# First feed-forward block: w1, w3 and gate in two passes that store w2's operands, then w2 alone as seven half-size products over all 1280 tokens

## The chip, the cores and the metric

The kernel runs on one core of a Trainium2 chip, one launch per execution. The metric is the time of one execution in microseconds (us). The kernel before takes 3238.82 us, the median of three runs from 3236.75 to 3240.59 us. The times of the rows below are of one profiled execution of it, which took 3245.91 us; the profile's span inside it is 3242.6 us, so that 3.3 us lie around the span.

## The reference

Two layers over 1024 latent tokens and 256 context tokens, D = 1024, all in fp32. Each layer has a mixer (layer 0: a state space beside latent attention; layer 1: retention beside HGRN2) and then a SwiGLU feed-forward block of 2816 hidden columns. The change is in the block of layer 0, where both streams are computed:

```python
def swiglu(h, w1, w3, w2):
    return (jax.nn.silu(h @ w1) * (h @ w3)) @ w2
...
        x = x + gx2 * swiglu(rms_norm(x, norm2_g[li]) * (1.0 + ax2) + sx2, ffn_w1[li], ffn_w3[li], ffn_w2[li])
        if not last:
            ...
            ctx = ctx + gc2 * swiglu(rms_norm(ctx, norm2_g[li]) * (1.0 + ac2) + sc2,
                                     ffn_w1[li], ffn_w3[li], ffn_w2[li])
```

The factors gx2 and gc2 (one number per column) are slices of the modulation vectors, one set for latent and one for context tokens. Behind this block comes the RMSNorm of layer 1, which every projection of layer 1 reads.

## The kernel before

**Numbers and products.** Every fp32 operand of a large product is split into a high and a low part (`split`, L175: ScalarE rounds the high part, L177; VectorE subtracts it, L43), and a product is three TensorE matmuls: high by high, high by low, low by high. Activations lie with features on the 128 partitions and tokens along the row. The 1280 tokens are held in two halves of 640: `x[0]` has 640 latent tokens, `x[1]` 384 latent and 256 context tokens (`HSEGS`).

**w1 and w3 as seven half-size products.** `Ffn.pair(j)` (L1292) does two of the 22 blocks of 128 hidden columns. Its 256 columns, the 1024 inputs and the 640 tokens of a half are each cut in two, and `seven` (L1243) makes the 2x2 block product from seven products of half size instead of eight (Strassen-Winograd). Each is 12 matmuls of 128x128 weights by 320 tokens (L1258). The seven sums of weights are cut for every pair (`wset`: four sums on GpSimd, seven splits of 512 columns); the seven sums of the input, the operands `ops` of 4x320, are cut once per half (`combos`, L1177, 14 pieces of 640). VectorE and GpSimd add up the results; `gate` multiplies silu(w1 part) by the w3 part, 128x320 at a time, and splits the result (`gh`, `gl`).

**w2 inside the pairs.** `Ffn.w2` (L1329) multiplies the gate of the pair before, 256 hidden columns deep, by the rows of w2: for 8 output blocks of 128 and two token segments (384 and 256) two times three matmuls, 96 in all (L215 to L217), and one `scalar_tensor_tensor` (L46) per output block and segment that scales the result and adds it to x. Thus x is read and written 11 times per half. The program issues it between the w1 and the w3 of the next pair; behind the last pair of a half it stands alone.

**Order.** The first pass does `x[0]`, the second `x[1]`. During the first, `prep` normalizes `x[1]` piece by piece; at the change of passes `combos` cuts the operands of the second pass, which takes the place of those of the first. During the second pass the sums of squares and the norm of `x[0]` for layer 1 are made; behind it stand the last w2, its sums of squares, and the norm of the first segment of `x[1]`; its second segment is normed after the first projection of layer 1. Beside the pairs TensorE also makes layer 1's modulation vectors (`mod_groups`, tile `psmod`). The order on each engine is set by a scheduler, except inside `tc.manual_schedule`, where the engines named take the program's order. SyncE (`Q`) issues all loads and stores, in one queue.

**The second block.** The block of layer 1 (1024 tokens) already works in the other way, with the class `Gate` (L1376): its `pair` does w1, w3 and the gate, sums the gate's four quarters into the seven operands of w2 on GpSimd, and hands each to `store`; behind the last pair w2 runs alone, as seven products over all its tokens, with its operands read back from DRAM.

## Time and profile before

| | us |
|---|---|
| median of three runs | 3238.82 |
| profiled execution | 3245.91 |
| span of the profile | 3242.6 |
| TensorE busy | 3045.4 (94% of the span) |
| VectorE busy | 2113.4 (65%) |
| GpSimd busy | 1352.8 (42%) |
| ScalarE busy | 1321.8 (41%) |
| first feed-forward block, first to last matmul | 858.9 to 1798.7: 939.8 |

The trace is read in microseconds from the span's start. Engines are PE (TensorE matmul), PEld (its weight loads, which overlap it), DVE (VectorE), ACT (ScalarE), POOL (GpSimd) and SP (SyncE). A row names the line of the kernel, the engine, the operation, and the tile written and the tiles read by the program's names. Tiles of `flat` that serve again keep their first names: `mh` and `ml` as outputs of a split, or as operands of a matmul, are in this block operands of `ops` or slots of the ring of weights. TensorE's busy time includes stretches in which the throttle granted it a lower clock; "granted clock" is the share of full speed.

### The profile page before, as it was taken

The numbers are of one execution on the slowest core, as the hardware profiler recorded it, in microseconds if no ns is written. First come the engines' busy times: TensorE is split into PE (matmuls) and PEld (weight loads), VectorE is DVE, ScalarE is ACT, GpSimd is POOL, SyncE is SP. The second block draws the span as 40 slices with busy tenths as digits, with TensorE's granted clock in tenths as the row PEclk, the third lists the DMA queues.
The fourth block names the chain that finished last, engine by engine and source line by source line (L and its number), as shares of the span: only waits on it lengthen the run. The fifth ranks groups of instructions, "written<-read, shape, count | busy, mean of one in ns | idle before, by whom it ended". The sixth has DMA issues, their size and how long they took to land.

```text
span 3242.6 us, 49888 instructions
## 1 busy us (share of the span) xinstructions
PE 3045.4 (94%) x19010; PEld 2727.4 (84%) x19010; DVE 2113.4 (65%) x3431; ACT 1321.8 (41%) x2643; POOL 1352.8 (42%) x1251
## 2 busy tenths in 40 slices
...
GB/s 247 271 162 112 17 19 28 115 163 189 124 118 111 111 116 99 140 108 118 104 118 66 66 33 33 40 43 40 40 44 197 98 95 102 103 101 102 332 214 140
DMA packets 168104, 363.10 MB, mean 112 GB/s; under 512 B 29865, under 2 KB 62265, under 8 KB 167097
## 3 DMA queue, kind: packets, MB, share of 16 engines
...
q14 instruction: 90, 0.74, 0.1%
...
## 4 chain that ended last, share of the span: by engine, by line
PE 67%; DVE 8%; issue 5%; POOL 4%; ACT 4%; DMA 2%; SPq 0%; POOLq 0%; ACTq 0%; DVEq 0%
PE psf L1412 13%; PE psf L1258 11%; PE psu L215 5%; PE psu L216 5%; PE psu L217 5%; PE psf L215 2%; PE psf L216 2%; PE psf L217 2%; PE pso L217 2%; PE pso L216 2%; PE pso L215 2%; PE psl L1751 2%; PE pso L2033 2%; PE pso L2035 2%; PE pso L2034 2%
## 5 line engine op out<-in xcount | busy, mean ns | idle before, releaser
L215 PE MATMUL psu<-mh,wh 128*128 128x384 f32 (+1 forms) x1024 | 327.3, 320 | 1.7 <-ACT qr L1629 1.2
L217 PE MATMUL psu<-mh,wl 128*128 128x384 f32 (+1 forms) x1024 | 323.8, 316 | 0.0
L216 PE MATMUL psu<-ml,wh 128*128 128x384 f32 (+1 forms) x1024 | 323.0, 315 | 0.0
L1412 PE MATMUL psf<-mix,ring 128*128 128x512 f32 x1248 | 295.7, 392 | 0.8 <-DVE c L43 0.8
L1412 PEld LDWEIGHTS psf<-mix,ring 128*128 128x128 f32 x1248 | 234.4, 188 | 53.2 <-DVE c L43 1.2
L43 POOL TENSOR_TENSOR fsum<-fraw,fsum 128x512 f32<-128x512 f32 x64 | 99.7, 1558 | 234.1 <-DVE ml L43 105.3
L215 PEld LDWEIGHTS psu<-mh,wh 128*128 128x128 f32 x1024 | 194.7, 190 | 2.2 <-ACT qr L1629 1.4
L216 PEld LDWEIGHTS psu<-ml,wh 128*128 128x128 f32 x1024 | 194.6, 190 | 0.1
L217 PEld LDWEIGHTS psu<-mh,wl 128*128 128x128 f32 x1024 | 194.3, 190 | 0.1
L46 DVE SCALAR_TENSOR_TENSOR x<-psf,mod,x 128x384 f32<-128x384 f32 (+1 forms) x352 | 175.1, 540 | 24.3 <-PE psf L217 20.7
L43 POOL TENSOR_TENSOR fsum<-fraw 128x512 f32<-128x512 f32 x75 | 108.1, 1442 | 130.8 <-DMA fraw<-ffn_w 99.7
L43 DVE TENSOR_TENSOR ml<-fraw,ml 128x512 fp32r<-128x512 f32 x132 | 125.7, 952 | 37.8 <-ACT ml L177 35.9
L43 POOL TENSOR_TENSOR s<-s,c 128x320 f32<-128x320 f32 x60 | 74.1, 1235 | 173.0 <-DVE c L43 164.3
L43 DVE TENSOR_TENSOR wx<-pT,wx 128x512 fp32r<-128x512 f32 x168 | 113.1, 682 | 33.4 <-ACT wx L836 33.4
L1258 PE MATMUL psf<-opx,mh 128*128 128x320 f32 x792 | 134.0, 310 | 0.8 <-DVE mh L43 0.8
L1412 PE MATMUL psf<-opx,ring 128*128 128x512 f32 x528 | 131.4, 393 | 2.2 <-ACT pu L1443 2.2
L829 ACT ACTIVATE pt<-pss,st 128x512 f32<-128x512 f32 (+1 forms) x208 | 123.5, 604 | 13.5 <-DVE st L817 11.5
L43 DVE TENSOR_TENSOR wl<-wraw,wh 128x1024 fp32r<-128x1024 f32 x61 | 90.4, 1481 | 59.0 <-ACT wh L177 49.0
L1258 PE MATMUL psf<-opx,ml 128*128 128x320 f32 x792 | 128.6, 310 | 0.2 <-DVE ml L43 0.2
L177 ACT CAST ml<-fraw 128x512 fp32r<-128x512 f32 x132 | 81.7, 619 | 111.0 <-PE psf L1258 33.7
L43 POOL TENSOR_TENSOR acc<-acc,sq 128x384 f32<-128x384 f32 (+2 forms) x57 | 71.7, 1264 | 132.3 <-ACT sq L1129 119.0
L43 POOL TENSOR_TENSOR xa<-xa,tot 128x1280 f32<-128x1280 f32 x24 | 87.2, 3634 | 90.2 <-ACT ku L1743 75.8
...
## 6 DMA issues: line engine op xcount, KB each, us to landing
...
```

The source lines that it names most:

```text
L43: return e.tensor_tensor(out=out, in0=in0, in1=in1, op=op)
L46: return V.scalar_tensor_tensor(out=out, in0=in0, scalar=scalar, in1=in1, op0=op0, op1=op1)
L177: S.copy(out=hi, in_=src)
L215: PE.matmul(ps, wh, xh, start=start, stop=False)
L216: PE.matmul(ps, wh, xl, start=False, stop=False)
L217: PE.matmul(ps, wl, xh, start=False, stop=stop)
L829: S.activation(out=o, in_=ps, func=AF.Exp, bias=st, accum_out=dd)
L1258: PE.matmul(ps, u[:, k], v[:, k], start=start and k == 0 and j == 0, stop=(k == 3 and j == 2), skip_group_check=True)
L1412: PE.matmul(ps(n), u[:, k], v[:, k], start=start and k == 0 and j == 0, stop=(k == 3 and j == 2), skip_group_check=True)
L1751: PE.matmul(ps[:, c], ku[:, c], qu, start=True, stop=True)
L2033: PE.matmul(o, wh, h, start=first, stop=False, skip_group_check=True)
L2034: PE.matmul(o, wh, l, start=False, stop=False, skip_group_check=True)
```

## The change

The class `Ffn` goes; the first block uses `Gate` as the second does. What each part does:

- **Pairs.** For each half and pair: w1 and w3 as seven products each, with products in the order 0, 5, 1, 3, 2, 4, 6. The gate runs on VectorE for all four quarters; GpSimd makes six sums of 128x320 a pair, two of results and four of the gate's quarters. Three quarters as they are and these four sums are w2's seven operands; each, 164 KB, is stored to a DRAM tile `g_d0` (154 stores in all; those of the very last pair are issued during w2's first product). No w2 in the pairs and no update of x.
- **Pass change.** The first weights of the second pass are cut between the pieces of `combos` (`get`), in the order in which the products take them.
- **w2.** Seven products over all 1280 tokens. The 2816 hidden columns come as 11 chunks j; each of products 0, 5, 1, 3, 2, 4 takes for each chunk one sum of w2's rows (`w2_op`, one split of 512) and one operand of 640 tokens (`x_op`: a load from `g_d0` and a split of 640), and runs 24 matmuls of 320 into eight PSUM banks (4 output blocks, 2 halves). The last three chunks go bank by bank, and behind each bank `put` adds the sum to x by `scalar_tensor_tensor`, once for each of the four quarters of a half that the product enters (`PUT`); in `x[1]`'s second 320 tokens as 64 latent and 256 context tokens. Product 6 runs the two halves one after the other. The sum t of the weights of products 1, 2, 3 is made in product 1, stored to `t_d` and read again in 2 and 3; its stores are issued two at a time.
- **Norms.** The sums of squares for layer 1 move into products 4 and 6; the norm of `x[0]` stands in the second half of product 6, both norms of `x[1]` behind layer 1's first projections of `x[0]` (two, then three column segments).
- **Order.** TensorE's and SyncE's orders in the w2 part are those of the program.

On TensorE, at the change from the first pass to the second. Before: `psf` by L1258 are w1 and w3 products, `gh` and `gl` the gate that w2 reads (L215, L216).

```order
L1258 MATMUL psf_12991<-mh_6900 128x320 x12
L1258 MATMUL psf_12990<-mh_6900,ml_6901 128x320 x12
L1258 MATMUL psf_12990<-ml_6901 128x320 x12
L215 MATMUL psf_13146<-gh_12697,mh_6900 128x384
L215 MATMUL psf_13147<-gh_12697,mh_6900 128x256
L215 MATMUL psf_13148<-gh_12697,mh_6900 128x384
L215 MATMUL psf_13149<-gh_12697,mh_6900 128x256
```

After (L1276 is the matmul of `Gate`; a product is twelve matmuls with one `psf`):

```order
L1276 MATMUL psf_11732<-opx_7473,mh_6900 128x320 x4
L1276 MATMUL psf_11492<-ml_6901,mh_6900 128x320 x12
L1276 MATMUL psf_11732<-ml_6901 128x320 x12
L1276 MATMUL psf_11760<-opx_7473,mh_6900 128x320 x2
L1276 MATMUL psf_11788<-opx_7473,ml_6901 128x320 x8
L1276 MATMUL psf_11613<-mh_6900 128x320 x12
L1276 MATMUL psf_11788<-opx_7473,ml_6901 128x320
L1276 MATMUL psf_11760<-opx_7473,mh_6900 128x320 x10
L1276 MATMUL psf_11788<-opx_7473,ml_6901 128x320 x3
L1276 MATMUL psf_11852<-opx_7473,ml_6901 128x320 x10
L1276 MATMUL psf_11613<-ml_6901 128x320 x12
L1276 MATMUL psf_11852<-opx_7473,ml_6901 128x320 x2
```

In the first listing the pass's last product is followed by matmuls of w2 on the last gate, so that TensorE has 96 of them between the passes; in the second the last product of the first pass is followed at once by products of the second.

On GpSimd, inside one pair. Before: `fsum` and `fraw` are sums of weights (512), `s`, `c` and `pu` sums of results (320).

```order
L43 TENSOR_TENSOR fsum_12565<-fraw_12563 128x512
L43 TENSOR_TENSOR fsum_12566<-fsum_12565,fraw_12561 128x512
L43 TENSOR_TENSOR fraw_12563<-fraw_12561,fraw_12563 128x512
L43 TENSOR_TENSOR fsum_12565<-fraw_12561,fsum_12566 128x512
L43 TENSOR_TENSOR s_12272<-pu_12306,pu_12304 128x320
L43 TENSOR_TENSOR fsum_12703<-fraw_12701 128x512
L43 TENSOR_TENSOR fsum_12704<-fsum_12703,fraw_12699 128x512
L43 TENSOR_TENSOR fraw_12701<-fraw_12699,fraw_12701 128x512
L43 TENSOR_TENSOR fsum_12703<-fraw_12699,fsum_12704 128x512
L43 TENSOR_TENSOR s_12272<-s_12272,c_12273 128x320
L43 TENSOR_TENSOR c_12273<-pu_12591,pu_12589 128x320
L43 TENSOR_TENSOR s_12272<-s_12272,c_12273 128x320
```

After (the same names; `c` holds sums of the gate as well):

```order
L43 TENSOR_TENSOR fsum_13096<-fraw_13084 128x512
L43 TENSOR_TENSOR s_12810<-s_12810,pu_12873 128x320
L43 TENSOR_TENSOR fsum_13100<-fsum_13096,fraw_13082 128x512
L43 TENSOR_TENSOR fraw_13084<-fraw_13082,fraw_13084 128x512
L43 TENSOR_TENSOR fsum_13096<-fraw_13082,fsum_13100 128x512
L43 TENSOR_TENSOR fsum_13234<-fraw_13088 128x512
L43 TENSOR_TENSOR c_12811<-c_12811,pu_13013 128x320
L43 TENSOR_TENSOR fraw_13088<-fraw_13086,fraw_13088 128x512
L43 TENSOR_TENSOR fsum_13238<-fsum_13234,fraw_13086 128x512
L43 TENSOR_TENSOR c_12811<-s_12810 128x320
L43 TENSOR_TENSOR s_12810<-s_12810 128x320
L43 TENSOR_TENSOR c_12811<-c_12811,s_12810 128x320
```

Each pair keeps its four sums of weights for w1 and four for w3; the sums of results with `pu` are fewer, and sums of the gate's quarters (`c` and `s` alone) stand between the sums of weights.

On SyncE, at the start of product 1 of w2. Before there is no such stage; the nearest is a pair, where rows of w2 are loaded between other weights.

```order
L1220 DMA fraw_16730<-ffn_w2 128x1024
L1220 DMA fraw_16732<-ffn_w2 128x1024
L1220 DMA fraw_16870<-w_mod 128x1024
L1220 DMA fraw_16872<-w_mod 128x1024
L1220 DMA fraw_16874<-w_mod 128x1024
L1220 DMA fraw_16888<-ffn_w3 128x1024
L1220 DMA fraw_16890<-ffn_w3 128x1024
```

After (`mh` here is a slot that takes a chunk's operand from `g_d0`; `t_d` takes the sums kept for products 2 and 3):

```order
L1379 DMA fraw_15506<-ffn_w2 128x2x512
L1380 DMA fraw_15507<-ffn_w2 128x512
L1496 DMA mh_6900<-g_d0_8576 128x640
L1379 DMA fraw_15543<-ffn_w2 128x2x512
L1380 DMA fraw_15544<-ffn_w2 128x512
L1496 DMA mh_6900<-g_d0_8576 128x640
L1531 DMA t_d_14754<-fsum_15509 128x512
L1531 DMA t_d_14754<-fsum_15546 128x512
L1379 DMA fraw_15582<-ffn_w2 128x2x512
L1380 DMA fraw_15583<-ffn_w2 128x512
```

A chunk of product 1 has two loads of w2 and one of an operand; two stores of t stand ahead of the loads of every second chunk.

```diff
...
                 split(S, ops[i][0][:, k], ops[i][1][:, k], src[:, k])
+            get(i)
 
         def sub(out, in0, in1):
             for k in kk:
         sub(b12, b12, b11)
         yield
         cut(0, b11)
+        cut(5, b21)
         cut(1, b12)
         sub(b12, b22, b12)
+        cut(3, b22)
         cut(2, b12)
         sub(b11, b12, b11)
-        cut(3, b22)
+        cut(4, b11)
         sub(b12, b21, b12)
-        cut(4, b11)
-        cut(5, b21)
         cut(6, b12)
-    class Ffn:
...
-        def pair(self, j):
...
-            self.w2()
...
-            def gate(i, v):
-                tt(G if i and j < NF // 2 - 1 else V, s[:, i], s[:, i], v, ALU.mult)
-                split(S, g[0][:, i], g[1][:, i], s[:, i])
...
     ORDER = (0, 5, 1, 3, 2, 4, 6)
     W2_ORDER = (0, 2, 5, 4, 1, 6, 3)
 
-    def w2_op(l, i, j, raw, fsum, slot, stash):
+    def w2_op(l, i, j, raw, fsum, slot, stash, keep=None):
         wh, wl = slot[:, 0:512], slot[:, 512:1024]
         w = a["ffn_w2"][l, 2 * j * P:(2 * j + 2) * P].rearrange("(f p) c -> p f c", p=P)
-        t = stash and stash[:, 512 * j:512 * j + 512]
         rr = lambda: raw().rearrange("p (f k) c -> p f (k c)", f=2)
         r = rr()
-        if i in (0, 5, 6, 1, 3):
+        if l == 0 and i in (1, 2, 3):
+            if i == 1:
+                r2, src, t = rr(), fsum(), fsum()
+                Q.dma_start(out=r, in_=w[:, :, 512:])
+                Q.dma_start(out=r2[:, 0], in_=w[:, 0, 0:512])
+                tt(G, src, r[:, 0], r[:, 1], ALU.add)
+                tt(G, t, src, r2[:, 0], ALU.subtract)
+                keep(j, t)
+            elif i == 2:
+                src = r[:, 0]
+                Q.dma_start(out=src, in_=stash[j])
+            else:
+                src = r[:, 0]
+                Q.dma_start(out=src, in_=w[:, 1, 0:512])
+                Q.dma_start(out=r[:, 1], in_=stash[j])
+                tt(G, src, src, r[:, 1], ALU.subtract)
...
     wp = tc.alloc_tile_pool(name="w5b", bufs=1, reuse_waits="tile")
-    f = Ffn(0, 320, HSEGS, ops, itertools.cycle(rs), wp, fr, pp,
-            lambda raw: mod_groups(1, raw, pp))
-    cb = combos(x[1], 320, ops, xs_d[1])
-    f.run(0, x[0], itertools.chain([0], prep(0, 3, 4, x[1], accs[1], HSEGS[1], xs_d[1], pp), itertools.islice(cb, 1)))
-    next(cb)
-    f.w2()
-    acc = Acc(xpool[0], HSEGS[0])
-    f.run(1, x[1], itertools.chain(stats(acc, HSEGS[0], x[0], wp),
-                                   prep(1, 0, 1, x[0], acc, HSEGS[0], x_d[:, :, 0:HALF[0]], pp)))
+    fraw = lambda: fr.tile([P, KT, P], F32, name="fraw", bufs=4)
+    f = Gate(0, 320, ops, itertools.cycle(rs), fraw)
+    f.pools(wp, wp, pp)
+    NJ = NF // 2
+    g_d = dram.tile([7, NJ, P, 2, 320], F32, name="g_d0")
+    fill = mod_groups(1, f.raw, pp)
+    store = lambda p, j: lambda i, v: Q.dma_start(out=g_d[i, j, :, p], in_=v)
+    w1 = [None]
+    cb = combos(x[1], 320, ops, xs_d[1], lambda i: w1[0].get(i))
+    mid = itertools.chain([0], prep(0, 3, 4, x[1], accs[1], HSEGS[1], xs_d[1], pp), itertools.islice(cb, 1))
+    kept = []
+    for p, j in itertools.product(range(2), range(NJ)):
+        keep = (lambda i, v: kept.append((i, v))) if p and j == NJ - 1 else store(p, j)
+        f.pair(j, keep, (w1[0], None), lambda: 0 < j < NJ - 1 and next(fill, None))
+        w1[0] = None
+        if p == 0:
+            next(mid, None)
+            if j == NJ - 1:
+                w1[0] = f.wset("ffn_w1", 0)
+                next(cb)
+    wp.release()
...
+    xslots = [itertools.cycle(v), itertools.cycle(v[6:]), itertools.cycle(slots([(bx, 0, 3200)], 640, 5))]
+    t_d = dram.tile([NJ, P, 512], F32, name="t_d")
     hh, hl = halves(HALF[0])
-    f.ring = iter(rs[6:])
-    w2 = f.w2_load()
-    for k in range(KT):
-        S.copy(out=hh[0][:, k], in_=x[0][:, k])
-        tt(G if k % 2 else V, hl[0][:, k], x[0][:, k], hh[0][:, k].bitcast(F32), ALU.subtract)
-    acc = Acc(xpool[0], HSEGS[1])
-    with tc.manual_schedule(engines={PE.engine}):
-        for i, d in itertools.product(range(2), range(KT)):
-            if i or d > 3:
-                f.w2_units(w2, [(i, d)])
-            elif d == 0:
-                f.w2_units(w2, [(0, j) for j in range(4)])
-            acc.add(i, x[1][:, d], d, wp, V if i else G)
-            if i == 1 and d == 4:
-                acc.col(0, pp)
-        pr = acc.bc(0, pp)
-    norm_apply(x[1], pr, 1, 0, 1, hh[1], hl[1], wp, HSEGS[1][0], "pu", PUB, XW)
-    Q.dma_start(out=x_d[:, :, HALF[0]:], in_=x[1])
+    NT = 3
+    accs = [Acc(wp, HSEGS[0], "b"), Acc(xpool[0], HSEGS[1])]
+    acc = accs[1]
+    PUT = {0: (1, 2, 3), 5: (0,), 1: (3,), 3: (1,), 2: (1,), 4: (3,), 6: (2,)}
+
+    def x_op(ring, src, n):
+        v = next(ring)
+        h, l = v[:, 0:n], v[:, n:2 * n]
+        Q.dma_start(out=l.bitcast(F32), in_=src)
+        split(S, h, l, l.bitcast(F32))
+        return h, l
+
+    def mms(o, w, xx, d, t0, first, last):
+        (wh, wl), (h, l) = [v[:, P * d:P * d + P] for v in w], [v[:, t0:t0 + 320] for v in xx]
+        PE.matmul(o, wh, h, start=first, stop=False, skip_group_check=True)
+        PE.matmul(o, wh, l, start=False, stop=False, skip_group_check=True)
+        PE.matmul(o, wl, h, start=False, stop=last, skip_group_check=True)
+
+    def put(o, u, d, p):
+        d, t0 = 4 * (u // 2) + d, 320 * (u % 2)
+        for c, n, m in ((0, 64, 0), (64, 256, 1)) if p and t0 else ((0, 320, 0),):
+            xk = x[p][:, d, t0 + c:t0 + c + n]
+            stt(xk, o[:, c:c + n], mod[:, 0, 5, m, d:d + 1], xk, ALU.mult, ALU.add)
+
+    def stat(p, i, ds, e=G):
+        for d in ds:
+            accs[p].add(i, x[p][:, d], d, wp, e)
+
+    with tc.manual_schedule(engines={PE.engine, Q.engine}):
+        for i in (0, 5, 1, 3, 2, 4):
+            if i in (0, 1, 2):
+                ps = [pp.tile([P, 512], F32, name="pso", tag="o", bufs=8)[:, :320] for _ in range(8)]
+            wx, late = [None] * NJ, []
+            for j in range(NJ):
+                wx[j] = (w2_op(0, i, j, fraw, fsum, next(wslots), t_d, lambda j, t: late.append((t_d[j], t))),
+                         x_op(xslots[i == 4], g_d[i, j].rearrange("p h t -> p (h t)"), 640))
+                if i == 0 and j == 3:
+                    late = [(g_d[u, NJ - 1, :, 1], t) for u, t in kept]
+                if i == 4 and j < 8:
+                    stat(j // 4, 0, [j % 4])
+                    stat(j // 4, 1, [j % 4])
+                if i == 0 or len(late) > 1 or j == NJ - 1:
+                    for o, t in late:
+                        Q.dma_start(out=o, in_=t)
+                    late = []
+                if j < NJ - NT:
+                    for b in range(8):
+                        mms(ps[b], *wx[j], b % 4, 320 * (b // 4), i in (0, 1, 2) and j == 0, False)
+            for b in range(8):
+                for j in range(NJ - NT, NJ):
+                    mms(ps[b], *wx[j], b % 4, 320 * (b // 4), False, i in (5, 3) and j == NJ - 1)
+                for u in PUT[i]:
+                    put(ps[b], u, b % 4, b // 4)
+        ws = []
+        for p in range(2):
+            xx = []
+            for j in range(NJ):
+                if p == 0:
+                    ws.append(w2_op(0, 6, j, fraw, fsum, next(wslots), None))
+                xx.append(x_op(xslots[2], g_d[6, j, :, p], 320))
+                if p == 0 and j < 8:
+                    stat(j // 4, 1, [4 + j % 4])
+                if p == 1 and j == 2:
+                    for i in range(2):
+                        accs[0].col(i, pp, "o", 8)
+                if p == 1 and j in (4, 5):
+                    norm_apply(x[0], accs[0].bc(j - 4, pp, "o", 8), 1, 0, 1, hh[0], hl[0], wp, HSEGS[0][j - 4], "pu", PUB, XW)
+                if j < NJ - 2:
+                    for d in range(4):
+                        mms(ps[4 * p + d], ws[j], xx[j], d, 0, False, False)
+            for d in range(4):
+                for j in (NJ - 2, NJ - 1):
+                    mms(ps[4 * p + d], ws[j], xx[j], d, 0, False, j == NJ - 1)
+                put(ps[4 * p + d], 2, d, p)
+                stat(p, 0, [4 + d], V)
+        for p in range(2):
+            Q.dma_start(out=x_d[:, :, HALF[0] * p:HALF[0] * (p + 1)], in_=x[p])
     wp.release()
     wf.release()
     fr.release()
```

## Rows read from the trace of the kernel before

**Rows 1.** The page: busy time of each engine; the chain of work, by engine.
```profile
PE 3045.4 (94%) x19010; PEld 2727.4 (84%) x19010; DVE 2113.4 (65%) x3431; ACT 1321.8 (41%) x2643; POOL 1352.8 (42%) x1251
...
PE 67%; DVE 8%; issue 5%; POOL 4%; ACT 4%; DMA 2%; SPq 0%; POOLq 0%; ACTq 0%; DVEq 0%
```

**Rows 2.** Windows (start:end, length, busy PE, PEld, DVE, ACT, POOL, clock, DMA, GB/s): block.
```profile
858.90:1798.70 939.80, 901.19 (x6259) 875.53 (x6259) 697.56 (x1119) 386.71 (x752) 438.02 (x318) 0.99 0.33 110
```

**Rows 3.** Windows, tile psmod alone, the same stretch.
```profile
858.90:1798.70 939.80, 24.45 (x384) 10.77 (x384) 2.20 (x6) 0.99 0.33 110
```

**Rows 4.** Timeline of PE: start, duration, then line, operation, tiles, form and count.
```profile
1750.85 0.28 PE L215 MATMUL psf<-gh,ml 128*128 128x256 f32 x1
...
1751.56 0.34 PE L215 MATMUL psf<-gh,ml 128*128 128x384 f32 x1
...
1752.08 0.33 PE L215 MATMUL psf<-gh,mh 128*128 128x384 f32 x1
...
1756.82 1.92 PE L1258 MATMUL psf<-opx,ml 128*128 128x320 f32 x12
...
1758.58 1.92 PE L1258 MATMUL psf<-opx,mh 128*128 128x320 f32 x12
```

**Rows 5.** Windows: pass change, end of the block, second block's pairs, its w2 part.
```profile
1280.00:1320.00 40.00, 26.86 (x153) 25.13 (x153) 38.22 (x45) 16.65 (x29) 23.62 (x14) 0.83 0.14 46
1760.00:1800.00 40.00, 28.83 (x179) 27.84 (x178) 30.29 (x47) 19.04 (x36) 18.41 (x13) 0.87 0.16 53
2600.00:2960.00 360.00, 360.00 (x1569) 294.38 (x1568) 185.28 (x247) 123.88 (x211) 189.09 (x132) 1.00 0.30 99
2985.00:3197.00 212.00, 203.40 (x857) 161.48 (x856) 163.58 (x180) 94.66 (x159) 102.99 (x66) 0.98 0.71 247
```

**Rows 6.** Timeline of PE, with the idle time before and what ended it.
```profile
1305.77 3.57 PE L1258 MATMUL psf<-ml 128*128 128x320 f32 x12 [9.48 <-DVE pu L43]
...
1313.83 0.44 PE L216 MATMUL psf<-gl,mh 128*128 128x384 f32 x1 [3.10 <-DVE gl L43]
...
1780.84 0.69 PE L216 MATMUL psf<-gl,mh 128*128 128x384 f32 x1 [6.98 <-DVE gl L43]
```

**Rows 7.** Groups of DVE by form, pass change (1270 to 1322): busy, mean ns | idle.
```profile
L43 DVE TENSOR_TENSOR opx<-x,opx 128x640 fp32r<-128x640 f32 x6 | 6.5, 1089 | 0.0
L43 DVE TENSOR_TENSOR mh<-x,mh 128x640 fp32r<-128x640 f32 x4 | 6.3, 1587 | 0.0
L43 DVE TENSOR_TENSOR ml<-x,ml 128x640 fp32r<-128x640 f32 x4 | 5.5, 1385 | 0.0
L43 DVE TENSOR_TENSOR mh<-fraw,mh 128x512 fp32r<-128x512 f32 x5 | 4.5, 904 | 0.0
```

**Rows 8.** Line L43 on DVE, pairs (1340 to 1740): count, min/median/max ns.
```profile
L43 DVE TENSOR_TENSOR ml<-fraw,ml x59: 673/693/1784, 1339.8 to 1736.4; 128x512 fp32r<-128x512 f32 x59
L43 DVE TENSOR_TENSOR pu<-pu,psf x40: 473/486/490, 1341.0 to 1737.8; 128x320 f32<-128x320 f32 x40
L43 DVE TENSOR_TENSOR gl<-s,gh x40: 476/492/1584, 1352.7 to 1739.1; 128x320 fp32r<-128x320 f32 x40
```

**Rows 9.** Line L43 on POOL, the same stretch.
```profile
L43 POOL TENSOR_TENSOR fsum<-fsum,fraw x19: 1279/1301/1750, 1369.0 to 1734.1; 128x512 f32<-128x512 f32 x19
L43 POOL TENSOR_TENSOR c<-pu x10: 869/882/1200, 1354.1 to 1729.8; 128x320 f32<-128x320 f32 x10
```

**Rows 10.** Timeline of DVE in the second block's w2 part.
```profile
3019.70 1.57 DVE L43 TENSOR_TENSOR mix<-stash,mix 128x512 fp32r<-128x512 f32 x1
3021.18 1.77 DVE L43 TENSOR_TENSOR opx<-opx 128x512 fp32r<-128x512 f32 x1
```

**Rows 11.** Timeline of POOL beside it.
```profile
3018.97 1.75 POOL L43 TENSOR_TENSOR stash<-fraw 128x512 f32<-128x512 f32 x1
3020.79 1.62 POOL L43 TENSOR_TENSOR stash<-stash,fraw 128x512 f32<-128x512 f32 x1
3022.37 1.74 POOL L43 TENSOR_TENSOR stash<-fraw 128x512 f32<-128x512 f32 x1
```

**Rows 12.** Groups of DVE by form, pairs (1340 to 1740).
```profile
L46 DVE SCALAR_TENSOR_TENSOR x<-psf,mod,x 128x384 f32<-128x384 f32 x72 | 43.6, 605 | 4.3 <-PE psf L217 4.2
L46 DVE SCALAR_TENSOR_TENSOR x<-psf,mod,x 128x256 f32<-128x256 f32 x72 | 34.0, 472 | 1.0
```

**Rows 13.** Windows: densest stretch of loads in the second block's w2 part.
```profile
3100.00:3120.00 20.00, 20.00 (x87) 16.11 (x87) 19.49 (x18) 10.21 (x18) 15.05 (x10) 1.00 0.96 361
```

More of the change, by code (lines that the diff above doesn't have):

```diff
@@ L1130, in add, with col, bc @@
                 tt(e, acc, acc, sq, ALU.add)
-        def col(self, i, pp):
-            self.rs[i] = rstd_col(self.acc[i], self.segs[i][1], 0, pp)
-        def bc(self, i, pp):
-            return rstd_bc(self.rs[i], self.segs[i][1], pp)
+        def col(self, i, pp, *tag):
+            self.rs[i] = rstd_col(self.acc[i], self.segs[i][1], 0, pp, *tag)
+        def bc(self, i, pp, *tag):
+            return rstd_bc(self.rs[i], self.segs[i][1], pp, *tag)
     MIXK = (4, 5, 6, 7, 0, 1, 2, 3)
@@ L1351, in get @@
             if i not in self.w:
+                if i in (2, 3):
+                    self.get(i - 1)
                 r1, r2 = self.r
@@ L1537, in slots @@
         return v[:c]
-    def stats(acc, segs, x, pool):
-        for d in range(0, KT, 2):
-            for d in (d, d + 1):
-                for i in range(len(segs)):
-                    acc.add(i, x[:, d], d, pool)
-            yield
     def mix2(*v):
```

138 lines of the change are left out of this document (18 added, 120 removed).

## The prediction

> **What bounds the kernel now.** I read the page first: TensorE is busy for 94% of the span and holds 67% of the chain of work, VectorE 8% [rows 1]. So a removed matmul is worth its time, unless another engine becomes late in its place. Then the window of the block that the change replaces: 939.8 us, TensorE busy 901.2, VectorE 697.6, GpSimd 438.0, granted clock 0.99 [rows 2]; 24.45 us of TensorE's time are the modulation vectors, which stay [rows 3]. The timeline gives the pace without gaps, from start to start: twelve matmuls of 320 in 1758.58 - 1756.82 = 1.76 us, 146.7 ns each; three of 384 in 0.52, 173.3 each; six of 256 in 0.71, 118.3 each [rows 4]. By the program there are 2 x 11 x 14 x 12 = 3696 matmuls of 320 (w1, w3) and 22 x 48 = 1056 each of 384 and 256 (w2): 542.2 + 183.0 + 124.9 = 850.1 us. What is left of the stage, 939.8 - 850.1 - 24.5 = 65.2 us, is idle time and lower clock. Two windows hold half of it. At the pass change TensorE did 153 matmuls in 40 us, worth 22.4 at 146.7 ns: 17.6 lost. At the end 179 in 40 us, worth 26.2: 13.8 lost [rows 5]. The waits there are for VectorE: 9.48 and 3.10 us, then 6.98 for the split of the last gate [rows 6]. The remaining 33.8 are about 1.5 us in each of 22 pairs.
>
> **Matmuls.** w2 becomes 7 products x 11 chunks x 24 = 1848 of 320 in place of 2112. After: 3696 + 1848 = 5544, times 146.7 ns = 813.3 us. 850.1 - 813.3 = **-36.8 us**. All of it lies on the engine that sets the end.
>
> **Pass change.** The order shows that w2 no longer stands between the passes; instead the second pass's products stand mixed behind the first's last ones. VectorE must make 14 cuts of 640 (6.5 + 6.3 + 5.5 = 18.3 us as stretched there), and beside them fourteen splits of weights at 0.904 = 12.7 [rows 7] and about eleven operations of 320 at 0.49 = 5.4 [rows 8]: 36.4 us. TensorE's cover, products whose operands are there already, is about 19 times 1.76 = 33.4. That leaves 3.0 of waiting. The slow clock cost the window before 26.86 busy - 22.4 = 4.4 [rows 5], and I leave that: 7.4, taken as 8 instead of 17.6: **-9.6**. Bounds: 3.6, and 17.6 if nothing is gained, since without w2's 96 matmuls (about 14 us) the cover is weaker by that much.
>
> **End.** The last gate's split and w2's first wait for it (6.98) go, since w2 starts with chunks stored long before. Late in its place is VectorE in the second half of product 6: the norm of x[0], twelve operations of 384 and twelve of 256 at 0.605 and 0.472 = 12.9 [rows 12], seven operand subtractions at 0.49 = 3.4, four puts at 0.54 (between the two sizes) = 2.2, eight sums of squares at about that = 4.3; in all 22.8. Beside it TensorE has seven chunks of twelve matmuls, 12.3, and layer 1's first segment, 24 of 384 at 173.3 ns, 4.2: 16.5. So 6.3 of waiting, and near 2 for the column sum ahead: 8 instead of 13.8, **-5.8**. Bounds 0 and 13.8.
>
> **w2 alone.** New, and to be bounded. The nearest row is the second block's w2, the same scheme: 203.40 busy of 212, 4.1% idle [rows 5]; of 271.1 us (1848 x 146.7 ns) that is **+11**. From below, one boundary by hand: behind product 0 each of 24 sums goes into x. 16 at 0.54 and 8 that are cut in 64 and 256 at 0.74 are 14.6 us of VectorE; it starts 1.3 after the eight banks' last 72 matmuls begin (10.6), and the next product reaches the eighth bank 3.1 later; 1.3 + 14.6 - 13.7 = 2.2. The other boundaries have 8 sums, 4.3 us, and fit. From above 25, if loading is late besides (second rival). I take 11, the measured row.
>
> **Pairs.** What goes: w2's 96 matmuls, 16 updates of x (0.605 and 0.472 [rows 12]), its four splits and the gate's three or four. What comes: seven stores of 164 KB and four sums on GpSimd. By the order a pair has on VectorE 14 splits of 512, 3 gate products with both inputs in SBUF, 9 operations that read PSUM: 14 x 0.693 + 3 x 0.492 + 9 x 0.486 = 15.6 us [rows 8]; on GpSimd 8 sums of 512 and 6 of 320: 8 x 1.301 + 6 x 0.882 = 15.7 [rows 9]. TensorE has 168 x 146.7 ns = 24.6 and 24.45 / 22 = 1.1 of modulation: 25.75. Both helpers fit; I leave the loss at 1.5 a pair, pitch 27.2 us, **0**. Bounds: the second block's pairs show no idle at all, 360.00 of 360 [rows 5], which would give back 33.8; and +79, third rival. The stores stand in SyncE's queue ahead of later loads and wait for GpSimd there; the second block does the same behind those 360 busy microseconds.
>
> **Sum.** -36.8 - 9.6 - 5.8 + 11 + 0 = -41.2. The profiled execution took 3245.9, of which 3.3 lie outside the span and stay: 3204.7. The median of the runs is 7.1 lower than that execution: **3198 us**.
>
> **Rivals.**
>
> First, VectorE and GpSimd exclude each other. In the pairs' rows VectorE's 512 split is 0.693 in the median and 1.784 at most, the operation that reads PSUM never above 0.490 [rows 8]; a GpSimd sum goes from 1.279 to 1.750 [rows 9]. So two inputs in SBUF collide with GpSimd. If they exclude each other for the whole operation, a pair needs 11.2 (14 splits, 3 gate products) + 15.7 = 26.9 us, over TensorE's 25.75: +1.2 x 22 = +25, 3223 us. Against it: where both are dense, two VectorE operations (1.57, 1.77 [rows 10]) and two of GpSimd (1.75, 1.62) take 3.40 us from 3018.97 to 3022.37 [rows 11]; one after the other, undisturbed, they would take 2 x 0.693 + 2 x 1.301 = 3.99. By 3.40 / 3.99 a pair needs 22.9, and fits. Chance 0.16. The Trainium skill states the stronger form ("SBUF — State Buffer", Who interferes with whom): an operation of VectorE with both inputs in SBUF and a GpSimd operation that reads SBUF lock each other out until the first ends. By that rule the time would be this rival's; the rows agree with which operations collide, not with the whole price.
>
> Second, w2's loads in product 1. By the order SyncE has two loads of w2 and one operand per chunk, and two stores of t, which wait for GpSimd, ahead of every second chunk's loads. Two chunks are 2.23 MB; at 361 GB/s, the densest window [rows 13], 6.2 us, and if the queue stands while GpSimd makes two sums, 3.4 [rows 11], 9.6 for two chunks where TensorE needs 7.0: 1.3 x 11 = +14, 3212 us. For it: the w2 window averages 247 GB/s already [rows 5]. Against: the slots let loads run several chunks ahead. Chance 0.12.
>
> Third, slower than before. VectorE loses every collision in the pairs: each of GpSimd's 14 sums holds one VectorE operation, and a held one takes (1.57 + 1.77) / 2 = 1.67 [rows 10], 0.98 above 0.693. Then VectorE needs 15.6 + 13.7 = 29.3 a pair and sets the pace over 25.75: +3.6 x 22 = +79, 3277 us. It decides from 10.4 held operations a pair, and makes the kernel slower from about 12.6, when a pair loses 2.15 us more than before. For it: the gate's four sums and the sums of weights now come in a shorter pair. Against: held operations are the exception in [rows 8], where the median (0.693) is near the minimum (0.673), with 13 GpSimd sums a pair. Chance 0.15: 0.11 slower, 0.03 in between.
>
> That the change does not do what it says can be left out: the order has 1848 matmuls of w2 and 3696 of w1 and w3.
>
> **Chances and range.** The forecast has 0.57, with an own range of 3175 to 3225 (pass change up to 9.6 worse, w2 up to 14 worse, pairs up to 20 better). Within 0.2% of 3238.8, about what a measurement of this kernel tells from no change, is 3232.3 to 3245.3. Faster: 0.54 of the forecast, 0.15 of the first rival, 0.12 of the second, 0.01 of the third: 0.82. Same: 0.02 + 0.01 + 0.03 = 0.06. Slower: 0.11 and 0.01 of the forecast's tail: 0.12. The range of 8 in 10 is 3172 to 3250: below lie pairs that give back most of their 1.5 us, above only the third rival's greater part.
>
> **What would show it.** Right: the block from first to last matmul about 900 us; 5544 matmuls of 320 at 1.76 per twelve; pairs about 27 us apart; the pass change with some 8 us lost, waiting for cuts; w2 about 282 us with 4% idle, a gap of 2 us behind product 0; some 8 us at the end, for the norm of x[0]. Wrong: a pitch over 28 with the 512 splits' mean near 1 us or more (first or third rival); gaps in product 1 that end with a DMA (second); no gain at the pass change because the cuts are stretched further.

## The result and the profile after

The changed kernel takes 3268.44 us (median of 4 runs, 3264.7 to 3276.18) against 3239.70 (4 runs): ratio 1.0092, 95% interval 1.0071 to 1.0113. It is slower by about 29 us, where 3198 was predicted: 70 us too low. Its profiled run took 3267.05 us, 62 over the 3204.7 that the sum gave for the profiled execution, so the traces can show nearly all of the miss.

The page's busy times and its chain, answering to [rows 1]:

```profile
PE 3032.5 (93%) x18746; PEld 2700.5 (83%) x18746; DVE 2104.8 (64%) x3229; ACT 1324.6 (41%) x2632; POOL 1441.8 (44%) x1326
...
PE 58%; DVE 10%; DMA 7%; POOL 6%; issue 5%; ACT 4%; SPq 1%; POOLq 0%; DVEq 0%; ACTq 0%
```

TensorE has 264 instructions less, and yet its share of the chain falls from 67% to 58%, while DMA, 2% before, has 7%. The removed matmuls are gone; something that is loaded has come onto the path.

The windows of the block (start:end, length, busy PE, PEld, DVE, ACT, POOL, clock, DMA, GB/s): pairs 1 to 9 of the first pass, the two pairs at the change, pairs 1 to 10 of the second, and w2; they answer to [rows 2, 5].

```profile
885.20:1150.00 264.80, 244.09 (x1711) 230.34 (x1711) 194.78 (x251) 104.37 (x207) 172.25 (x128) 0.99 0.49 159
...
1150.00:1224.90 74.90, 60.23 (x338) 57.60 (x337) 63.92 (x68) 31.34 (x58) 52.84 (x35) 0.86 0.37 122
...
1224.90:1516.90 292.00, 271.89 (x1881) 256.39 (x1880) 217.81 (x272) 113.81 (x224) 184.19 (x138) 0.98 0.47 154
1516.90:1817.50 300.60, 283.65 (x1869) 278.82 (x1869) 183.31 (x278) 117.75 (x205) 96.74 (x75) 0.96 0.62 211
```

The block lasts from 855.9 to 1817.4, 961.5 us, where 939.8 - 41.2 = 898.6 were forecast. With the first pair (29.3) the twenty pairs outside the change take 586.1 us, 29.3 each, where 27.2 were forecast: +42. The change of passes takes 74.9 for two pairs, forecast 62.4 (two times 27.2 and 8): +12.5. w2 takes 300.6, forecast 290 with the end (271.1 + 11 + 8): +10.5. Together these are 65 us, about the 62.9 by which the block is over its forecast.

**Pairs.** TensorE's waits from 885.2 to 1516.9 (line waited at, what for; us, times, longest):

```profile
PE psmod L141 <- DMA fraw<-w_mod: 22.7, 13, 3.4
PE psf L1276 <- DVE s L43: 8.4, 5, 3.2
PE psf L1276 <- ACT s L1348: 6.0, 3, 3.0
PE psf L1276 <- DVE c L43: 5.2, 7, 3.0
```

The largest is not for VectorE or GpSimd, which all the rivals on the pairs spoke of. It is for the modulation weights of layer 1, which the change did not touch; before (885.2 to 1760), the same wait was 1.0 us:

```profile
PE psmod L141 <- DMA fraw<-w_mod: 1.0, 2, 0.6
```

This view counts the time in which no matmul is shown as running. The gaps named from here on are counted from start to start, as the time beyond the pace without gaps, wherever it is over 0.2 us. So counted, the nineteen pairs behind the first and outside the change lose 31.2 us ahead of `psmod` (before, in the nearest windows, 1.4) and 28.7 ahead of w1's and w3's products (before about 19, of which 14 stood ahead of w2's matmuls). The SyncE queue of one such group of loads, and TensorE at the same place:

```profile
1004.18 2.37 SPq L1251 DMA_DIRECT2D fraw<-w_mod  x2
1010.82 0.33 SPq L1459 DMA_DIRECT2D g_d<-s  x1
1013.26 0.33 SPq L1459 DMA_DIRECT2D g_d<-c  x1
1013.68 0.99 SPq L1459 DMA_DIRECT2D g_d<-s  x2
1015.64 0.32 SPq L1459 DMA_DIRECT2D g_d<-c  x1
1017.89 0.33 SPq L1251 DMA_DIRECT2D fraw<-w_mod  x1
1018.32 0.38 SPq L1251 DMA_DIRECT2D fraw<-ffn_w  x1
```

```profile
1021.77 1.50 PE L141 MATMUL psmod<-fraw,cst 128*32 128x256 f32 x24 [3.28 <-DMA fraw<-w_mod]
```

Two of the group's three loads go at 1004, the third 14 us later; five stores of the gate stand between them, and the third load also takes a buffer that w3's weights must first leave. TensorE stands 3.28 us. SyncE's own waits in the first pass (885 to 1150) name both: the stores (L1459) wait for the gate, the loads (L1251) for raw buffers that the sums and splits still read.

```profile
SPq L1459 <- DVE s L43: 56.1, 20, 7.1
SPq L1251 <- POOL fsum L43: 45.8, 15, 9.2
SPq L1251 <- DVE ml L43: 44.7, 10, 8.0
```

Before, the queue's waits for such buffers were longer still in the same window (130.8 and 96.2 us for VectorE's splits of `mh` and `ml`), and TensorE felt next to nothing of them. So a long wait of the queue is not yet a loss; the experiments have to say which of the two is one.

**w2.** From the timeline, the seven products take 38.7, 44.8, 49.7, 48.8, 38.7, 38.7 and 41.3 us. 264 matmuls at 146.7 ns are 38.7: products 0, 2 and 4 lose nothing at all, and but for 2.6 us in product 6 all of the loss is at the second, third and fourth place (products 5, 1, 3). SyncE's stores of t in product 1, and TensorE's one long wait:

```profile
1583.34 3.87 SPq L1531 DMA_DIRECT2D t_d<-fsum  x2
...
1594.97 3.86 SPq L1531 DMA_DIRECT2D t_d<-fsum  x2
...
1606.64 3.80 SPq L1531 DMA_DIRECT2D t_d<-fsum  x2
```

```profile
1609.48 0.63 PE L1502 MATMUL pso<-mh 128*128 128x320 f32 x1 [7.99 <-DVE x L46]
```

Each pair of stores comes 11.6 us after the one before; two chunks need 7.0 us on TensorE. GpSimd, in between, first waits for the loads and then makes four sums, two for each chunk, from 1592.30 to 1598.49; of these the first and the last are

```profile
1592.30 1.28 POOL L43 TENSOR_TENSOR fsum<-fraw 128x512 f32<-128x512 f32 x1 [5.42 <-DMA fraw<-ffn_w]
...
1596.73 1.76 POOL L43 TENSOR_TENSOR fsum<-fsum,fraw 128x512 f32<-128x512 f32 x1
```

The queue stands until they are done, and only then do the next loads go: 5.4 us of waiting for loads and 6.2 of sums are the 11.6. TensorE's wait is put down to an update of x on VectorE, but that update stood in VectorE's order behind a split whose sum was still to be loaded: it hides a late DMA.

### The profile page after: what moved, and what is told of

It is laid out like the page before. It is cut to its first block, busy times and chain, and to the rows that moved or that the text cites. A ratio compares the mean times of both kernels' runs of the same rounds, so it can differ in the third digit from the quotient of the medians.

```text
span 3265.1 us, 49941 instructions
## 1 busy us (share of the span) xinstructions
PE 3032.5 (93%) x18746; PEld 2700.5 (83%) x18746; DVE 2104.8 (64%) x3229; ACT 1324.6 (41%) x2632; POOL 1441.8 (44%) x1326
## 4 chain that ended last, share of the span: by engine, by line
PE 58%; DVE 10%; DMA 7%; POOL 6%; issue 5%; ACT 4%; SPq 1%; POOLq 0%; DVEq 0%; ACTq 0%
PE psf L1276 16%; PE psu L215 5%; PE psu L216 4%; PE psu L217 4%; DMA fraw<-ffn_w 3%; PE pso L1502 2%; DVE mh L43 2%; PE pso L1503 2%; PE pso L1504 2%; POOL fsum L43 2%; DVE ml L43 2%; PE pso L217 2%; PE pso L216 2%; PE psl L1710 2%; PE pso L215 2%
## 5 line engine op out<-in xcount | busy, mean ns | idle before, releaser
L215 PE MATMUL psu<-mh,wh 128*128 128x384 f32 (+1 forms) x1024 | 328.5, 321 | 1.3 <-ACT mh L196 0.8
L216 PE MATMUL psu<-ml,wh 128*128 128x384 f32 (+1 forms) x1024 | 324.2, 317 | 0.6 <-POOL ml L43 0.6
L1276 PE MATMUL psf<-mix,ring 128*128 128x512 f32 x1248 | 295.6, 392 | 0.8 <-DVE c L43 0.8
L1276 PEld LDWEIGHTS psf<-mix,ring 128*128 128x128 f32 x1248 | 234.4, 188 | 53.2 <-DVE c L43 1.2
L43 POOL TENSOR_TENSOR fsum<-fraw 128x512 f32<-128x512 f32 x97 | 144.4, 1491 | 257.2 <-DMA fraw<-ffn_w 195.9
L215 PEld LDWEIGHTS psu<-mh,wh 128*128 128x128 f32 x1024 | 195.8, 191 | 2.0 <-ACT mh L196 1.1
L216 PEld LDWEIGHTS psu<-ml,wh 128*128 128x128 f32 x1024 | 195.8, 191 | 1.0 <-POOL ml L43 0.9
L43 DVE TENSOR_TENSOR mh<-fraw,mh 128x512 fp32r<-128x512 f32 x113 | 125.7, 1113 | 59.9 <-ACT mh L177 58.0
L43 POOL TENSOR_TENSOR fsum<-fraw,fsum 128x512 f32<-128x512 f32 x64 | 95.2, 1487 | 145.4 <-DVE ring L43 93.4
L1276 PE MATMUL psf<-opx,mh 128*128 128x320 f32 x792 | 144.7, 318 | 14.1 <-ACT s L1348 6.0
L1276 PEld LDWEIGHTS psf<-opx,mh 128*128 128x128 f32 x792 | 124.4, 193 | 20.1 <-ACT s L1348 6.8
L43 DVE TENSOR_TENSOR wl<-wraw,wh 128x1024 fp32r<-128x1024 f32 x61 | 89.4, 1466 | 72.7 <-ACT wh L177 62.6
L43 DVE TENSOR_TENSOR wx<-pT,wx 128x512 fp32r<-128x512 f32 x168 | 113.0, 681 | 32.3 <-ACT wx L836 32.2
L1276 PE MATMUL psf<-opx,ring 128*128 128x512 f32 x528 | 131.4, 393 | 2.2 <-ACT pu L1307 2.2
L1276 PE MATMUL psf<-opx,ml 128*128 128x320 f32 x792 | 133.1, 310 | 0.3 <-ACT ml L177 0.3
L829 ACT ACTIVATE pt<-pss,st 128x512 f32<-128x512 f32 (+1 forms) x208 | 123.3, 603 | 13.6 <-DVE st L817 11.6
L43 POOL TENSOR_TENSOR xa<-xa,tot 128x1280 f32<-128x1280 f32 x24 | 87.2, 3633 | 90.4 <-ACT ku L1702 76.0
L836 ACT CAST wx<-pT 128x512 fp32r<-128x512 f32 x168 | 96.2, 592 | 68.3 <-PE pT L834 68.3
L43 DVE TENSOR_TENSOR ml<-fraw,ml 128x512 fp32r<-128x512 f32 x113 | 108.1, 958 | 24.1 <-ACT ml L177 22.6
L43 POOL TENSOR_TENSOR fsum<-fsum,fraw 128x512 f32<-128x512 f32 x75 | 112.0, 1494 | 25.8 <-DVE ring L43 13.0
```

The costliest lines, as they stand in the source:

```text
L43: return e.tensor_tensor(out=out, in0=in0, in1=in1, op=op)
L215: PE.matmul(ps, wh, xh, start=start, stop=False)
L216: PE.matmul(ps, wh, xl, start=False, stop=False)
L829: S.activation(out=o, in_=ps, func=AF.Exp, bias=st, accum_out=dd)
L836: S.copy(out=ph, in_=pT)
L1276: PE.matmul(ps(n), u[:, k], v[:, k], start=start and k == 0 and j == 0, stop=(k == 3 and j == 2), skip_group_check=True)
```

## The experiments

Two causes offered themselves for the pairs: A, SyncE's queue (loads behind stores that wait for the gate), and C, the four raw buffers that w1, w3 and the modulation weights use in turn. B is the third rival of the prediction, collisions of VectorE and GpSimd. All were timed beside the kernel before on the same chip, whose medians were 3243.48, 3246.54 and 3244.82 in the three groups. The changed kernel was not timed again in them, so the ratio to the kernel before is the fair comparison; that of the changed kernel is 1.0092 (1.0071 to 1.0113).

**e1, the gate's stores on ScalarE's queue.**

```diff
-    store = lambda p, j: lambda i, v: Q.dma_start(out=g_d[i, j, :, p], in_=v)
+    store = lambda p, j: lambda i, v: S.dma_start(out=g_d[i, j, :, p], in_=v)
```

> The changed kernel with one edit: the 154 stores of the gate's sums are issued by ScalarE's queue instead of SyncE's. Theory A (modulation weights come late because their loads stand in SyncE's queue behind stores that wait for the gate; TensorE stands about 31 us before psmod in the pairs): these gaps fall from 31 to under 10 us, time 3268 - 22 = about 3246 us. Theory B (VectorE and GpSimd collide in the pairs and come late): same collisions, 3268 within 5 us. Theory C (the four raw buffers, which weights and modulation weights share, are what the loads wait for): the gaps stay near 31, 3268 within 5 us; or more, if ScalarE is now held by the stores.

3261.96 us, ratio 1.0059 (1.0044 to 1.0074): by the ratio about a third of the loss goes, but the two intervals touch. The gaps ahead of `psmod` fall only from 31.2 to 21.5, where A wanted under 10. A is a part at most.

```profile
PE psmod L141 <- DMA fraw<-w_mod: 16.7, 9, 3.7
```

**e7, the modulation matmuls without priority.**

```diff
-                with tc.high_priority(offset=GROUP):
+                with tc.high_priority(offset=0):
```

> The changed kernel with one edit: the modulation matmuls lose the priority that puts them ahead in TensorE's order, so that they stand later behind their loads. A and C both expect the psmod gaps (31 us) to fall under 10 and the time to about 3245. B expects no change, 3268 within 5 us. Later matmuls hold the raw buffers longer; if C holds strongly, part of the gain comes back as later splits of weights: 3255.

3268.72 us, 1.0084 (1.0068 to 1.0099). A miss for A and C alike: 22.6 us of gaps stay. The edit did not do what it was meant to: groups that stood behind the eighth or ninth of a pair's 14 products now stand behind the fifth to ninth, on the whole not later. So it tells nothing of why the loads are late.

**e6, the gate's sums on VectorE.** The four `tt(G, ...)` of `gate` become `tt(V, ...)` in this block.

> The changed kernel with one edit: the four sums of the gate's quarters per pair run on VectorE instead of GpSimd (14 GpSimd operations a pair become 10). Theory B: VectorE's 512 splits fall from a mean of 1.06 us toward 0.85 and the stores come earlier; VectorE gives 14 x 0.2 = 2.8 back for 4 x 0.49 = 2.0 us more, the pairs fall by 1 to 2 us each, 3268 - 20 to 40 = about 3238. Theory A: what is late stays late, since the first quarter's store still waits for the gate; 3268 within 6 us.

3269.87 us, 1.0079 (1.0063 to 1.0096). GpSimd has 88 operations less. VectorE's 512 splits do get shorter, from 1.08 to 0.91 us in the mean over the nineteen pairs, 46 us in all; but the gate's sums, now on VectorE, bring operations of 320 that take 52 us more, and nothing is gained. The waits for VectorE's own results grow:

```profile
PE psf L1276 <- DVE s L43: 13.7, 7, 4.9
PE psf L1276 <- DVE c L43: 12.9, 12, 2.2
PE psmod L141 <- DMA fraw<-w_mod: 11.9, 10, 3.6
```

B's gain of 20 to 40 us did not come. But since VectorE got as much new work as it was spared, this alone does not rule B out.

**e11, w3's loads behind the modulation loads,** the turn of the kernel before; the same four buffers.

```diff
-            ws = [w or self.wset(n, j) for n, w in zip(("ffn_w1", "ffn_w3"), ws)]
+            box = [ws[0] or self.wset("ffn_w1", j), ws[1] or (None if mid else self.wset("ffn_w3", j))]
+            ws = [types.SimpleNamespace(get=lambda i, u=u: box[u].get(i)) for u in range(2)]
...
             for u in range(2):
+                box[u] = box[u] or self.wset("ffn_w3", j)
```

> The changed kernel with one edit: in the first block w3's two loads of a pair are issued behind the modulation loads, as in the kernel before, not at the pair's start. Same four buffers, another turn: the modulation loads now follow buffers of the pair before. Theory C: psmod gaps fall from 31 to under 10; but w3's loads now wait for modulation buffers, which may give 10 us back in waits of w3's products; time 3250 to 3258. Theory A: gaps stay, 3268 within 5 us.

3247.18 us, ratio 1.0011 (0.9996 to 1.0026). The gaps ahead of `psmod` are 9.0, as C said, though stores and loads still share the queue:

```profile
PE psmod L141 <- DMA fraw<-w_mod: 7.3, 9, 2.2
```

The turn in which loads take the buffers is worth some 25 us. What this run does not separate is the place of the modulation matmuls: most of them stand behind the eighth of a pair's products in the changed kernel, and here behind the thirteenth or the last, so that their loads also have longer to come.

**e9, modulation weights in buffers of their own.**

```diff
-    fill = mod_groups(1, f.raw, pp)
+    def mraw(src):
+        r = wp.tile([P, KT, P], F32, name="mraw", bufs=3)
+        Q.dma_start(out=r.rearrange("p k c -> p (k c)"), in_=src)
+        return r
+    fill = mod_groups(1, mraw, pp)
```

> The changed kernel with one edit: the modulation weights get three raw buffers of their own, in place of the four that they share with w1 and w3. Theory C (in the changed pair w1 and w3 take all four buffers at its start, so the third modulation load of a group waits for w3's first buffer, and the next pair's w1 for the rest): TensorE's gaps before psmod (31 us in the pairs) fall to under 6 and the time by 25 to 30, to about 3242. Theory A (SyncE's queue behind the stores, which ScalarE's queue took away only in part): gaps stay at 15 or more, 3268 - 10.

3220.82 us, ratio 0.9928 (0.9904 to 0.9952): faster than the kernel before, and a gain of 48 us by the medians where C wanted 25 to 30. Gaps ahead of `psmod` are 1.6 us, and those of w1's and w3's products, which C did not count, fall from 28.7 to 18.6: these loads no longer stand behind modulation weights in the ring either. The twenty pairs outside the change take 540.4 us instead of 586.1, 27.0 each, as forecast.

```profile
PE psmod L141 <- DMA mraw<-w_mod: 1.3, 2, 0.7
```

Modulation is done early, and eight later pairs without it, 1235 to 1440, run at 25.6 us each:

```profile
1235.00:1440.00 205.00, 199.49 (x1346) 197.13 (x1345) 179.90 (x210) 90.01 (x178) 154.65 (x112) 1.00 0.39 129
```

VectorE is busy for 179.9 of 205, 22.5 a pair, with the same instructions as in the changed kernel. Its groups there (busy, mean ns):

```profile
L43 DVE TENSOR_TENSOR mh<-fraw,mh 128x512 fp32r<-128x512 f32 x32 | 37.8, 1181 | 1.0 <-ACT mh L177 0.4
L43 DVE TENSOR_TENSOR ml<-fsum,ml 128x512 fp32r<-128x512 f32 x24 | 31.3, 1304 | 10.2 <-ACT ml L177 8.6
...
L43 DVE TENSOR_TENSOR s<-pu,psf 128x320 f32<-128x320 f32 x25 | 12.0, 478 | 0.0
```

The collisions are all there. The four groups of 512 splits take 1.12 us in the mean here; in the pairs of before (1340 to 1740) the same four took 0.89; two of them were

```profile
L43 DVE TENSOR_TENSOR ml<-fraw,ml 128x512 fp32r<-128x512 f32 x59 | 58.1, 985 | 23.4 <-ACT ml L177 22.2
L43 DVE TENSOR_TENSOR mh<-fraw,mh 128x512 fp32r<-128x512 f32 x59 | 46.4, 786 | 2.8 <-ACT mh L177 2.1
```

Over the nineteen pairs the mean is 1.06, nearly the 1.08 of the changed kernel, while these pairs became 47.5 us shorter. So collisions are not what made the pairs longer than forecast. That settles B.

**e20, e9 with the gate's stores on ScalarE's queue** (the edits of e9 and e1).

> The run with own modulation buffers (3221 us) with one edit more: the gate's 154 stores by ScalarE's queue. Theory C alone (buffers, not the queue, made the loads late): 3221 within 5 us, pairs at the same pace of 25.6. Theory A as a second cause of its own: another 5 to 10 us less, since the first run with these stores moved was about 7 us below the changed kernel.

3225.63 us, ratio 0.9937 (0.9915 to 0.9959), no better than e9: with buffers free, the stores in SyncE's queue cost nothing that shows. That they cost something in e1's comparison fits loads that had no slack there.

**e4, the stores of t on ScalarE's queue.**

```diff
                     for o, t in late:
-                        Q.dma_start(out=o, in_=t)
+                        (Q if i == 0 else S).dma_start(out=o, in_=t)
```

> The changed kernel with one edit: in w2's product 1 the stores of t are issued by ScalarE's queue. Theory A for w2 (the loads of two chunks stand behind two stores that wait for GpSimd, which gives a period of 11.6 us for two chunks where TensorE needs 7.0): the period falls to about 8.5, the wait of 8.0 us before product 1 to under 3 and the product from 49.7 to about 42; time 3268 - 9 = about 3259. Rival D (the period is that of the loads and GpSimd's sums themselves): period stays above 11, 3268 within 4 us. Rival E (ScalarE, now held by the stores, delays its own casts): product 1 longer than 49.7, time up.

3260.31 us, ratio 1.0060 (1.0039 to 1.0082). Product 1 falls from 49.7 to 46.6, not to the 42 hoped for, and product 3 from 48.8 to 38.7. The time alone shows little, since its interval overlaps that of the changed kernel; the products show it. TensorE's waits for updates of x in w2 fall from 16.9 us to

```profile
PE pso L1502 <- DVE x L46: 7.0, 6, 1.8
```

The second rival's mechanism is shown. Product 5 keeps its loss (46.2): its waits are for the updates of x behind product 0, the boundary worked out by hand.

**e14, three edits: e9, e4, and product 0's last five chunks bank by bank.**

```diff
-                if j < NJ - NT:
+                if j < NJ - (5 if i == 0 else NT):
...
-                for j in range(NJ - NT, NJ):
+                for j in range(NJ - (5 if i == 0 else NT), NJ):
```

> Three edits together: own buffers for modulation weights, stores of t by ScalarE's queue in product 1, and product 0's last five chunks (not three) bank by bank. By theory C and by the run with the stores of t moved, the first two are worth 25 and 13 us. The third gives TensorE 8 x 15 matmuls, 17.6 us, beside product 0's 24 updates of x, 14.6 us on VectorE: product 5 (44.8 us, of which 38.7 are matmuls) falls to about 40. Sum: 3268 - 25 - 13 - 5 = 3225, faster than the kernel before. If VectorE's updates are not what product 5 waits for, it stays at 45 to 47 and the time is about 3230.

3205.17 us, ratio 0.9878 (0.9857 to 0.9899). The products take 38.7, 43.6, 38.7, 38.7, 38.7, 38.7, 41.4; product 1 is now without loss: its last loads of w2 begin at 1553.4, 2 us ahead of its first matmul, where in e4 they began 0.8 us behind it. Of the 5 us hoped for from the third edit, 1 to 3 came in product 5 (44.8 in the changed kernel, 46.2 in e4); whether the last 8 us of product 1 are due to it as well is not separated. The time is 20 us under the 3225 expected, as e9's edit was worth 48 us and not 25. w2's window:

```profile
1473.00:1751.50 278.50, 275.44 (x1870) 274.57 (x1869) 181.07 (x278) 117.67 (x205) 93.60 (x75) 0.99 0.67 228
```

**e18, e14 with the subtractions between the cuts on VectorE.**

```diff
-                tt(G, out[:, k], in0[:, k], in1[:, k], ALU.subtract)
+                tt(V, out[:, k], in0[:, k], in1[:, k], ALU.subtract)
```

> The fastest version so far (3205 us: own modulation buffers, t stored by ScalarE's queue, five chunks bank by bank) with one edit: the subtractions of 640 between the cuts of the pass change (and those ahead of the first pass) run on VectorE instead of GpSimd. If collisions with GpSimd stretch the cuts (0.81 us alone, 1.3 to 1.5 in the mean there), the cuts' mean falls to about 1.0 and pays for the eight operations of 0.82 that VectorE takes over: the pass change, 73.2 us for two pairs, falls to about 68, time 3200. If VectorE's own work is the bound there, it gets longer: 76, time 3208.

3196.44 us, ratio 0.9857 (0.9833 to 0.9881), the fastest; its interval overlaps e14's, so that the gain is read from one trace of each: the two pairs at the change take 64.4 us instead of 73.2, and GpSimd is busy for 40.0 of them instead of 51.5. VectorE's cuts there, first e14 (1141 to 1215), then e18 (1135 to 1215):

```profile
L43 DVE TENSOR_TENSOR opx<-x,opx 128x640 fp32r<-128x640 f32 x6 | 7.6, 1274 | 0.0
L43 DVE TENSOR_TENSOR mh<-x,mh 128x640 fp32r<-128x640 f32 x4 | 6.4, 1599 | 0.0
L43 DVE TENSOR_TENSOR ml<-x,ml 128x640 fp32r<-128x640 f32 x4 | 6.2, 1561 | 0.0
```

```profile
L43 DVE TENSOR_TENSOR opx<-x,opx 128x640 fp32r<-128x640 f32 x6 | 6.7, 1115 | 0.0
L43 DVE TENSOR_TENSOR x<-x 128x640 f32<-128x640 f32 x6 | 5.1, 869 | 0.0
L43 DVE TENSOR_TENSOR mh<-x,mh 128x640 fp32r<-128x640 f32 x4 | 5.0, 1247 | 0.0
L43 DVE TENSOR_TENSOR ml<-x,ml 128x640 fp32r<-128x640 f32 x4 | 4.5, 1112 | 0.0
```

VectorE takes six operations more and does the cuts faster: over the fourteen the mean falls from 1.44 to 1.16 us, with less of GpSimd's work beside them.

Not tried: the kernel before with buffers of its own for the modulation. What they would be worth there stays open; its own wait for these weights was 1.0 us.

## Why the prediction was wrong

- **Matmuls, -36.8: right.** 5544 matmuls of 320, and wherever nothing is late a product of w2 takes 38.7 us, 264 x 146.7 ns.
- **Pairs, "0": the step that failed.** I left the loss at 1.5 us a pair and wrote that stores in SyncE's queue do no harm since the second block has them "behind those 360 busy microseconds". That row was no evidence: in the stretch of [rows 5] no modulation weights are loaded between the pairs. Here three loads a pair go through the same four buffers, and `Gate` takes all four at the pair's start where `Ffn` took w3's two only after them. The prediction counted each instruction on VectorE and GpSimd and none of the loads' buffers: it put the wait for loads in the pairs at nothing. It cost 42 us: some 30 ahead of `psmod`, the rest ahead of w1 and w3. e9, with buffers of their own, brings the pairs to the pitch that was forecast; e11, another turn in the same buffers, brings 25 us; e1, whose gaps ahead of `psmod` fall to 21.5, points to the stores ahead of these loads as a part of it, as long as the ring has no slack.
- **Collisions (first and third rival): real, not the cause.** The third rival's 3277 lies near the time measured, but by chance. VectorE needs 22.5 us a pair (e9), not the 15.6 counted from medians nor the 29.3 of the rival; TensorE needs 24.6. A sum of work wants means: that of a 512 split was 0.89 already before, not 0.693. e9 reaches the forecast pitch with the collisions in it.
- **The first rival's rows were misread.** In [rows 10, 11] the second VectorE operation begins at 3021.18 and takes 1.77, so it ends at 3022.95, when a third GpSimd operation has begun: the four operations take 3.98 us and not 3.40, about the 3.99 that they would take one after the other. These rows thus agree with the rule quoted there. That the whole of every operation is exclusive does not fit e9, though: with the shortest durations of [rows 8, 9] the colliding operations of a pair add up to 26.3 us, an estimate, and e9's eight pairs take 25.6.
- **Pass change, -9.6: nothing gained.** The upper bound came true and more: two pairs take 74.9, of which 49.3 are matmuls: 25.6 lost, about 17 in gaps and the rest at a lower pace, with a granted clock of 0.86. TensorE's waits there (1150 to 1251) are, by name, for VectorE's sums and the gate, hardly for cuts:

```profile
PE psf L1276 <- DVE s L43: 6.4, 2, 3.2
PE psf L1276 <- DVE c L43: 3.6, 3, 3.0
PE psf L1276 <- ACT s L1348: 3.0, 1, 3.0
```

  The 14 cuts (1150 to 1225) take 20.4 us where 18.3 were put:

```profile
L43 DVE TENSOR_TENSOR opx<-x,opx 128x640 fp32r<-128x640 f32 x6 | 8.2, 1387 | 0.0
L43 DVE TENSOR_TENSOR mh<-x,mh 128x640 fp32r<-128x640 f32 x4 | 6.9, 1737 | 0.0
...
L43 DVE TENSOR_TENSOR ml<-x,ml 128x640 fp32r<-128x640 f32 x4 | 5.3, 1326 | 0.0
```

  So the cuts by themselves are 2 us of the miss. By the prediction's durations VectorE has 18.3 + 2 x 15.6 = 49.5 us of work in the two pairs; it is busy for 63.9, as splits and sums are stretched too, and the sums for which TensorE waits stand in its order behind cuts and splits: the sum that ends a wait of 3.22 at 1180.0 follows two cuts (2.20 and 0.81) and two splits. GpSimd is busy for 52.8 of 74.9 us beside it, 71%, where before it was 23.6 of 40, 59% [rows 5]; and e18, which only moves GpSimd's subtractions away from that place, gives 9 us back. How the rest of the 25.6 divides stays open.
- **w2, +11: mis-sized, 27.** The second rival, put at a chance of 0.12, took place on top of the forecast, and dearer: 11.6 us for two chunks instead of 9.6, since GpSimd makes four sums for them and not two, and the queue stands until these are done and only then begins to load. Products 1 and 3 lose 21.1 us by it; e4 takes 13 of them away, e14 all. The boundary behind product 0 was forecast at 2.2 and costs 6.1, 4.9 when given longer cover.
- **End, -5.8: about right.** Product 6 takes 2.6 us over its matmuls. The rest comes behind the block, beside layer 1's first segments, which the prediction had in its cover: from the block's last matmul to the 385th of layer 1's projections it is 67.0 us, before 60.5. The longest wait there (1776.3 to 1840) is for a sum of squares, ahead of the column sum:

```profile
PE pcol L160 <- DVE acc L43: 2.8, 1, 2.8
```

  Together 9.1 us where 8 were allowed. By the end of the execution 3.8 of these 6.5 us are left, and ahead of the block the changed kernel is 3.0 us earlier; why, no run shows.

With the loads' buffers, t's stores, product 0's last chunks and the cuts' neighbour changed, the same design takes 3196.44 us, about what the sum gave. That the figures meet is in part chance. In e18's trace the pairs take 27.1 us each and the change of passes 64.4, near the forecast of 27.2 and 62.4; w2 with the end takes 279 where 290 were forecast, and what lies behind the block 6 us more than before.
